# Linear attention with queries, keys and log decays projected in transposed form, block totals summed on VectorE, and the two-half products ordered tile by tile

## The chip, the cores and the metric

The kernel runs on one core of a Trainium2 chip. The metric is the device time in microseconds (us) of one execution; lower is better. TensorE does the matrix products, VectorE and ScalarE the arithmetic on rows, GpSimd some helpers, and SyncE issues all transfers.

## The reference, cut to what matters

One step of a two-layer backbone. In each layer a projection `h @ w_in` feeds three branches (grouped-query attention, gated linear attention, latent attention), their gates, and a merge. The change is in the linear attention (four heads, key width 64, value width 128, two directions, 1024 latent and 128 context tokens):

```python
qg = qg.reshape(bsz, n, GLA_HEADS, GLA_DK) * (GLA_DK ** -0.5)
la_f = jax.nn.log_sigmoid((rf @ p['w_gla_decay_fwd'] + p['b_gla_decay_fwd']))
la_b = jax.nn.log_sigmoid((rb @ p['w_gla_decay_bwd'] + p['b_gla_decay_bwd']))
...
def step(s, inp):
    qc, kc, vc, gc = inp
    cum = jnp.cumsum(gc, axis=1)
    last = cum[:, -1]
    o_inter = jnp.einsum('bchk,bhkv->bchv', qc * jnp.exp(cum), s)
    decay = jnp.exp(jnp.where(mask, cum[:, :, None] - cum[:, None, :], -jnp.inf))
    att = jnp.einsum('bihk,bjhk,bijhk->bhij', qc, kc, decay)
    s_new = jnp.exp(last)[..., None] * s + jnp.einsum('bjhk,bjhv->bhkv', kc * jnp.exp(last[:, None] - cum), vc)
```

## The kernel before

Tokens are nine tiles of 128. Every large product is made of three TensorE matmuls (`mm3`, lines 85 to 87), on a high and a low part of each factor. A layer runs in stages.

**Projection units.** `nat` puts tokens on partitions: a unit of 256 columns of `w_in` is 9 tiles x 8 k-steps x 3 matmuls with 256 moving columns. `trn` puts features on partitions: a unit of 128 columns is 3 chunks x 8 x 3 matmuls with 384 moving columns. `gla_unit` 0 and 1 make queries and keys with `nat`, 2 and 3 the values, all written to the scratch tensor `glas`. `decay` makes the log decays with tokens on partitions, and `decay2` finishes them and stores them in `las`.

**The scan.** `t_unit` makes the transposed gate projections (36 a layer). Class `Gla` hands out the linear attention of four heads in small steps, one after each twelve `mm3` matmuls of a `t_unit`, until the heads are done. Two chains of heads run side by side, the second `LAG` steps behind. Later `t_unit`s run without the scan, so the scan's TensorE work is added to that of the `t_unit`s, which does not depend on it.

A head (`head`, line 713) keeps rows of a tile with keys on partitions: the half `up` (partitions 0 to 63) and the half `dn` (64 to 127), one for each direction. It loads `la` and `qk`; line 735 multiplies the decays with the constant `blk` to get the totals of blocks of 1, 2, 4, up to 128 tokens, and lines 738 and 739 exponentiate them into `one` and `tot`; lines 751, 754 and 755 transpose queries and keys into `zb` and `za`. Then come six levels of widening blocks: line 793 for widths 1 to 16, line 809 for 32, line 820 for 64. In each, products of the `up` half go to a PSUM bank from `pst` and those of the `dn` half to a bank from `acc`; `join` then multiplies `za` and `zb` by the block decays on VectorE. The order of the first kind was:

```python
for pc, ks, qs, rows, f in ((banks[0], za, zb, up, 1), (banks[1], zb, za, dn, 0)):
    for t in range(NT):
        for b, bs in enumerate(quarters):
```

Line 837 turns the keys back into `kh` with tokens on partitions, line 847 makes the states' updates, lines 869 and 871 the output, line 885 transposes it.

**The rest.** Attention follows, then the merge and the output projection. The order on each engine is set by a scheduler from the order of the code and its own estimates; the engines run their lists in order, and the pools (three PSUM banks `f` for the units, two `acc`, three `pst`) set when a result's room is free. A matmul on full 32-bit data stands as two rows in the trace, one of `mm3` as one.

Of the kernel before, what the change touches and what calls it, by code (L numbers as in the profile page):

```python
# [20 lines left out]
P = 128  # L21
# [7 lines left out]
NCH = 3  # L29
# [17 lines left out]
def hybrid_step(ctx, tc, a):  # L47
# [174 lines left out]
    with ExitStack() as st:  # L222
        xs = enter(st, "hx0", 2)
        xT = xs.tile([P, KD, T], F32, tag="xT", name="xT", bufs=1)
        for t in range(NT):
            x32 = xs.tile([P, D], F32, tag="x", name="x", bufs=3)
            sp.dma_start(x32, x_rows(0, t))
            for hf, pt in to_t(pa["pst"], x_norm(xs, x32)):
                (act.copy, dve.tensor_copy)[hf](xT[:, hf * 4:hf * 4 + 4, t * P:(t + 1) * P], pt)
        loads = []  # L230
        for hf in range(2):
            def load(k):
                w = xs.tile([P, 2, 512], F32, tag="wm", name="wm", bufs=4)
                src = a["w_mod"][0, k * P:(k + 1) * P, 0:2 * D].rearrange("p (j c) -> p j c", j=2)
                loads.append(sp.dma_start(w, src[:, :, 512 * hf:512 * (hf + 1)]))
                return w.rearrange("p j c -> p (j c)")

            for step in mod_steps(0, [(j, 512 * hf, 512) for j in range(2)], pa[("f", "acc")[hf]], xs, load):
                step()
            if hf:  # L240
                last = loads[-1]
                with tc.issue_after(loads[9].ins):
                    first = load_unit(0, QG, pool)
# [21 lines left out]
    for l in range(DEPTH):  # L265
# [10 lines left out]
        glas = dr.tile([P, NT, 1024], F32, tag=f"glas{l}", name="glas")  # L276
        las = dr.tile([P, NT, 512], F32, tag=f"las{l}", name="las")
# [38 lines left out]
        with ExitStack() as st:  # L316
# [3 lines left out]
            def gla_unit(i, beside=None):  # L320
                hi, lo = first if l == 0 and i == 0 else load_unit(l, QG + 256 * i, dve)
                for t in range(NT):
                    if l or i:
                        pc = accf()
                    elif t % 2 == 0:
                        pair = (accf if t < 6 else pa["acc"])()
                        pc = pair
                    else:
                        pc = pair[:, 256:]
                    nat(pc[:, :256], t, hi, lo)  # L330
                    z = zp.tile([P, 256], F32, tag="zg", name="zg")
                    act.activation(z, pc[:, :256], AF.Copy, scale=1.0 if i else 0.125)  # L332
                    sp.dma_start(glas[:, t, 256 * i:256 * (i + 1)], z)
                    if beside:
                        beside(t)
                    elif i:
                        tick()

            gla_unit(0)
# [33 lines left out]
            u = n1.tile([P, NT, 512], F32, tag="u", name="u")  # L373
            mn = n1.tile([P, NT, 512], F32, tag="mn", name="mn")
# [3 lines left out]
            def decay(t):  # L378
                pc = accf()
                pe.matmul(pc, lhsT=rT[:, t * P:(t + 1) * P], rhs=wd.rearrange("p h b d -> p (h b d)"),  # L380
                          start=True, stop=True)
                act.activation(u[:, t], pc, AF.Abs)
                act.activation(u[:, t], u[:, t], AF.Exp, scale=-1.0)
                dve.tensor_scalar(mn[:, t], pc, 0.0, 1.0 / 16.0, op0=ALU.min, op1=ALU.mult)
# [10 lines left out]
            def decay2(t):  # L395
                rope_key(t, kr[:, t])
                if t % 3 == 2:
                    ts = slice(t - 2, t + 1)
                    act.activation(u[:, ts], u[:, ts], AF.Ln, bias=1.0)
                    dve.scalar_tensor_tensor(mn[:, ts], u[:, ts], -1.0 / 16.0, mn[:, ts], op0=ALU.mult, op1=ALU.add)  # L400
                    sp.dma_start(las[:, ts], mn[:, ts])

            gla_unit(1, decay)
            gla_unit(2, decay2)
            gla_unit(3)
# [112 lines left out]
        def t_unit(nm, c0, i, fill=None, beside=None):  # L518
            hi, lo = wunit(KD, P, [(0, P, a["w_in"][l, :, c0 + P * i:c0 + P * (i + 1)])], dve if beside else pool)
            for ch in range(NCH):  # L520
# [5 lines left out]
                if nm[0] != "m":  # L526
# [5 lines left out]
        env = dict(small=small, ident=ident, identr=identr, rstd=rstd, tri=tri, msk=msk,  # L532
                   twos=twos, wp=wp, wunit=wunit, cosm=cosm, sinm=sinm, split=split, mm3=mm3, glas=glas, las=las,
# [134 lines left out]
class Gla:  # L668
# [7 lines left out]
    def __init__(self, st, tc, enter, a, l, e):  # L676
# [7 lines left out]

        self.blk = self.g1.tile([P, 2 * P - 1], F32, tag="blk", name="blk")
        for w in BLOCKS:
            self.nc.vector.tensor_tensor(self.blk[:, OFF[w]:OFF[w] + P // w], e["tri"][:, 0, w - 1::w],
                                         e["tri"][:, 2, 0::w], op=ALU.mult)
# [24 lines left out]
    def head(self, h):  # L713
        nc, e, a, l, g1, g2, wide = self.nc, self.e, self.a, self.l, self.g1, self.g2, self.wide
        pe, act, dve, pool, sp = nc.tensor, nc.scalar, nc.vector, nc.gpsimd, nc.sync
        acc, pst, ident, blk = e["acc"], e["pst"], e["ident"], self.blk
# [3 lines left out]
        la = wide([NT, P], "la")  # L720
        sp.dma_start(la, e["las"][:, :, P * h:P * h + P])
        qk = wide([NT, 2, 64], "qk")
        for b in range(2):
            sp.dma_start(qk[:, :, b], e["glas"][:, :, 256 * b + 64 * h:256 * b + 64 * h + 64])
# [3 lines left out]
        one = wide([NT, P], "one")  # L728
        tot = wide([NT, P - 1], "tot")
        for t0 in range(0, NT, 2):  # L730
            n = min(2, NT - t0)
            pt = pst()[:, :n * (2 * P - 1)]
            for i in range(n):
                for rows in (up, dn):
                    pe.matmul(pt[rows, i * (2 * P - 1):(i + 1) * (2 * P - 1)], lhsT=la[:, t0 + i, rows], rhs=blk,  # L735
                              start=True, stop=True)
            pv = tiles(pt, n)
            act.activation(one[:, t0:t0 + n], pv[:, :, 0:P], AF.Exp)
            act.activation(tot[:, t0:t0 + n], pv[:, :, P:], AF.Exp)
            if t0 % 4:  # L740
                yield
        decay = lambda w: tot[:, :, OFF[w] - P:OFF[w] - P + P // w]
        yield

        za = wide([NT, P], "za")
        zb = wide([NT, P], "zb")
        for t0 in range(0, NT, 3):
            pa, pb = acc(), pst()
            for t in range(3):
                c = slice(t * P, (t + 1) * P)  # L750
                pe.transpose(pb[:, c], qk[:, t0 + t].rearrange("p b d -> p (b d)"), ident)
            for t in range(3):
                c = slice(t * P, (t + 1) * P)
                pe.matmul(pa[up, c], lhsT=qk[:, t0 + t, 1], rhs=ident, start=True, stop=True)
                pe.matmul(pa[dn, c], lhsT=qk[:, t0 + t, 0], rhs=ident, start=True, stop=True)
            act.copy(zb[:, t0:t0 + 3], tiles(pb[:, 0:3 * P], 3))
            act.copy(za[:, t0:t0 + 3], tiles(pa[:, 0:3 * P], 3))
            yield
# [14 lines left out]
        sp.dma_start(vn, e["glas"][:, :, 512 + P * h:512 + P * h + P])  # L773
# [5 lines left out]
        def join(w):  # L779
            d = one if w == 1 else decay(w)  # L780
            d = d.rearrange("p t (n f) -> p t n f", f=2)
# [24 lines left out]
        for b, bs in enumerate(quarters):  # L806
            ks, qs, rows = ((za, zb, up), (zb, za, dn))[b % 2]
            for t in range(NT):
                pe.matmul(banks[b % 2][bs, t * 32:t * 32 + 32], lhsT=ks[rows, t, bs], rhs=qs[rows, t, quarters[b ^ 1]],
                          start=True, stop=True, tile_position=(rows.start, 32 * b))  # L810
# [5 lines left out]
        for t0, n in ((0, 5), (5, 4)):  # L816
            banks = [pst()[:, 0:n * 64], acc()[:, 0:n * 64]]
            for pc, ks, qs, rows, other in ((banks[0], za, zb, up, dn), (banks[1], zb, za, dn, up)):
                for t in range(n):
# [13 lines left out]
        for t0, n in ((0, 4), (4, 4), (8, 1)):  # L833
            pc = pst()[:, 0:n * P]
            for t in range(n):
                for x, r in ((za, up), (zb, dn)):
                    pe.matmul(pc[:, t * P + r.start:t * P + r.stop], lhsT=x[:, t0 + t], rhs=ident[:, r],  # L837
                              start=True, stop=True)
            act.copy(kh[:, t0:t0 + n], tiles(pc, n))
            if t0 != 4:  # L840
                yield
# [642 lines left out]
```

## Time and profile before

| what | value |
|---|---|
| median of 3 runs | 3094.7 us (3093.02 to 3095.74) |
| the profiled execution's own time | 3095.74 us |
| its span, first to last instruction | 3094.0 us |
| TensorE busy | 3038.7 us, 98% |
| VectorE busy | 1579.4 us, 51% |
| ScalarE busy | 1154.8 us, 37% |
| scan of layer 0, and of layer 1 | about 366 to 728 us, and 1872 to 2234 us |

The span is 1.7 us shorter than the execution. Matmuls are pipelined and their ends are modelled, so that the length of one is not its cost: its cost is the distance to the start of the next.

### The profile page before, as it was taken

The numbers are of one execution on the slowest core, as the hardware profiler recorded it, in microseconds if no ns is written. First come the engines' busy times: TensorE is split into PE (matmuls) and PEld (weight loads), VectorE is DVE, ScalarE is ACT, GpSimd is POOL, SyncE is SP. The second block draws the span as 40 slices with busy tenths as digits, with TensorE's granted clock in tenths as the row PEclk, the third lists the DMA queues.
The fourth block names the chain that finished last, engine by engine and source line by source line (L and its number), as shares of the span: only waits on it lengthen the run. The fifth ranks groups of instructions, "written<-read, shape, count | busy, mean of one in ns | idle before, by whom it ended". The sixth has DMA issues, their size and how long they took to land.

```text
span 3094.0 us, 63128 instructions
## 1 busy us (share of the span) xinstructions
PE 3038.7 (98%) x25776; PEld 2673.5 (86%) x25776; DVE 1579.4 (51%) x2789; ACT 1154.8 (37%) x2412; POOL 750.2 (24%) x780
## 2 busy tenths in 40 slices
PE   7999999999999999999999999999999999999998
PEld 5989999999999666699899999999999976667997
DVE  5325543332078667757542473433213876786562
ACT  5523433333212565522345343333331245554121
POOL 3124300002200555500331460000130125553012
PEclk8999999999999999999999999999999999999999
DMA  7565522326343432186433444232463442214843
GB/s 238 175 191 160 142 76 82 100 82 187 112 119 102 133 94 78 33 258 210 152 102 116 119 114 122 88 96 75 123 178 98 123 140 91 78 52 139 276 140 109
DMA packets 389347, 394.72 MB, mean 128 GB/s; under 512 B 53740, under 2 KB 333804, under 8 KB 388928
## 3 DMA queue, kind: packets, MB, share of 16 engines
q1 hardware_dynamic: 389056, 390.67, 41.4%
q8 instruction: 203, 3.33, 0.5%
q14 instruction: 88, 0.72, 0.1%
HBM read 258.07 MB, written 113.64 MB: 120 GB/s over the span
## 4 chain that ended last, share of the span: by engine, by line
PE 93%; DVE 3%; ACT 1%; DMA 1%; issue 1%; SPq 0%; POOL 0%; ACTq 0%; DVEq 0%; POOLq 0%
PE f L85 18%; PE f L87 18%; PE f L86 18%; PE acc L1347 4%; PE acc L86 4%; PE acc L85 3%; PE acc L87 3%; PE pst L1089 3%; PE s L1214 2%; PE s L1215 2%; PE s L1172 1%; PE pst L735 1%; PE pst L837 1%; PE s L1174 1%; PE s L1173 1%; PE pst L793 1%
## 5 line engine op out<-in xcount | busy, mean ns | idle before, releaser
L85 PE MATMUL f<-big,whi 128*128 128x384 f32 x1776 | 609.1, 343 | 0.8 <-ACT zg L332 0.5
L87 PE MATMUL f<-big,wlo 128*128 128x384 f32 x1776 | 602.4, 339 | 0.7 <-issue 0.7
L86 PE MATMUL f<-big,whi 128*128 128x384 f32 x1776 | 600.4, 338 | 0.0
L85 PE MATMUL f<-whi,big 128*128 128x256 f32 (+1 forms) x1352 | 394.4, 292 | 1.2 <-ACT big L98 0.8
L87 PE MATMUL f<-whi,big 128*128 128x256 f32 (+1 forms) x1352 | 394.1, 292 | 0.8 <-DVE big L99 0.6
L86 PE MATMUL f<-wlo,big 128*128 128x256 f32 (+1 forms) x1352 | 392.7, 291 | 0.7 <-POOL wlo L99 0.7
L85 PEld LDWEIGHTS f<-big,whi 128*128 128x128 f32 x1776 | 333.7, 188 | 8.5 <-issue 6.4
L87 PEld LDWEIGHTS f<-big,wlo 128*128 128x128 f32 x1776 | 333.4, 188 | 3.9 <-issue 3.3
L86 PEld LDWEIGHTS f<-big,whi 128*128 128x128 f32 x1776 | 333.9, 188 | 1.8 <-issue 1.5
L99 DVE TENSOR_TENSOR wlo<-raw,whi 128x1024 fp32r<-128x1024 f32 (+3 forms) x116 | 141.7, 1222 | 348.7 <-ACT whi L98 186.2
L1102 ACT ACTIVATE pr<-s 128x512 f32<-128x512 f32 x440 | 247.8, 595 | 184.8 <-PE s L1215 111.7
L1107 POOL TENSOR_TENSOR sm<-sm,pr 128x512 f32<-128x512 f32 x192 | 264.9, 1393 | 179.8 <-DVE sm L1107 92.6
L85 PEld LDWEIGHTS f<-whi,big 128*128 128x128 f32 x1352 | 254.5, 188 | 15.6 <-issue 7.9
L87 PEld LDWEIGHTS f<-whi,big 128*128 128x128 f32 x1352 | 254.6, 188 | 7.3 <-DVE big L99 1.3
L86 PEld LDWEIGHTS f<-wlo,big 128*128 128x128 f32 x1352 | 254.6, 188 | 6.6 <-POOL wlo L99 1.2
L98 ACT CAST whi<-raw 128x1024 fp32r<-128x1024 f32 (+2 forms) x150 | 154.3, 1029 | 282.3 <-PE f L86 242.7
L1091 DVE TENSOR_REDUCE nm<-pst 128x1 f32<-128x384 f32 x480 | 239.5, 551 | 33.1 <-PE pst L1089 22.8
L99 POOL TENSOR_TENSOR wlo<-raw,whi 128x1024 fp32r<-128x1024 f32 x34 | 81.5, 2397 | 403.9 <-ACT whi L98 395.0
L1107 DVE TENSOR_TENSOR sm<-sm,pr 128x512 f32<-128x512 f32 x144 | 132.5, 924 | 87.7 <-POOL sm L1107 50.0
L525 ACT ACTIVATE g<-f 128x384 f32<-128x384 f32 x144 | 70.4, 489 | 285.3 <-PE f L87 197.6
L92 POOL TENSOR_SCALAR rm<-oss 128x9 f32<-128x9 f32 x8 | 1.7, 207 | 614.9 <-ACT sq L875 614.9
L99 DVE TENSOR_TENSOR lo<-pr,hi 128x512 fp32r<-128x512 f32 (+1 forms) x148 | 145.4, 1005 | 3.6 <-ACT hi L98 3.4
(329 smaller groups left out, 6063.2 us busy)
## 6 DMA issues: line engine op xcount, KB each, us to landing
raw<-in_w_in SPq DMA_DIRECT2D x108, 512.0 KB
gtm<-g SPq DMA_DIRECT2D x144, 192.0 KB
sg<-gtm SPq DMA_DIRECT2D x144, 192.0 KB
wm<-in_w_mod SPq DMA_DIRECT2D x48, 512.0 KB
big<-y SPq DMA_DIRECT2D x96, 192.0 KB
glas<-zg SPq DMA_DIRECT2D x72, 128.0 KB
gqT<-stg SPq DMA_DIRECT2D x36, 256.0 KB
gqa<-gqT SPq DMA_DIRECT2D x36, 256.0 KB
```

The lines of the kernel that those rows point to most:

```text
L85: pe.matmul(out, lhsT=lh, rhs=rh, start=first, stop=False)
L86: pe.matmul(out, lhsT=lh, rhs=rl, start=False, stop=False)
L87: return pe.matmul(out, lhsT=ll, rhs=rh, start=False, stop=last)
L98: act.copy(hi, src)
L99: lo_eng.tensor_tensor(lo, src, hi.bitcast(F32), op=ALU.subtract)
L525: act.activation(th, pc[:, :CH], AF.Tanh, scale=0.5)
L1089: r = nc.tensor.matmul(pc[:, :CH], lhsT=q[:, t * P:(t + 1) * P], rhs=k[:, j * CH:(j + 1) * CH], start=True, stop=True)
L1091: nc.vector.reduce_max(nm[:, t, j:j + 1], pc[:, :CH], axis=AX.X)
L1102: self.nc.scalar.activation(pr, pc, AF.Exp, scale=scale)
L1107: eng.tensor_tensor(s_, x, y, op=ALU.add)
L1214: pe.matmul(pc, lhsT=self.kah[g][:, ks], rhs=qa, start=True, stop=False)
L1347: after = nc.tensor.matmul(po[64 * j:64 * j + 64], lhsT=at.gv[:, kt, g], rhs=pr, start=j not in begun, stop=kt == GROUPS[-1][0])
```

## The change

Queries and keys of a head come from one `trn` unit (64 query and 64 key columns, `qk_unit`, four a layer), with features on partitions, and are stored in `qkT`. The decays are made with features on partitions too (12 matmuls of 384 columns for 9 of 512). A head loads `one`, `zb` and `za` as it needs them; the constant `blk`, its products and the transposes are gone. Block totals are made by seven additions on VectorE, each from pairs of the one before, and two ScalarE instructions exponentiate all of them. In the levels, and where the keys are turned back, the tile loop is outside and the half inside; the keys are turned back with 64 rows at a time, one bank for each half.

```diff
-            gla_unit(0)
+            def qk_unit(h, beside):
+                hi, lo = wunit(KD, P, [(64 * i, 64, a["w_in"][l, :, c + 64 * h:c + 64 * h + 64])
+                                       for i, c in enumerate((QG, KG))], dve)
+                for ch in range(NCH):
+                    pc = accf()
+                    trn(pc[:, :CH], ch, hi, lo)
+                    z = n2.tile([P, CH], F32, tag="zt", name="zt")
+                    act.activation(z[0:64], pc[0:64, :CH], AF.Copy, scale=0.125)
+                    dve.tensor_copy(z[64:128], pc[64:128, :CH])
+                    sp.dma_start(qkT[:, h, ch * CH:(ch + 1) * CH], z)
+                    beside(NCH * h + ch)
...
-            gla_unit(1, decay)
-            gla_unit(2, decay2)
-            gla_unit(3)
+            v_unit(1, key)
+            for h in range(4):
+                qk_unit(h, finish)
...
-                    pe.matmul(pt[rows, i * (2 * P - 1):(i + 1) * (2 * P - 1)], lhsT=la[:, t0 + i, rows], rhs=blk,
-                              start=True, stop=True)
...
+        for w in BLOCKS[1:]:
+            x = decay(w // 2).rearrange("p t (n f) -> p t n f", f=2)
+            dve.tensor_tensor(decay(w), x[:, :, :, 0], x[:, :, :, 1], op=ALU.add)
+        for x in (one, tot):
+            act.activation(x, x, AF.Exp)
...
-            for pc, ks, qs, rows, f in ((banks[0], za, zb, up, 1), (banks[1], zb, za, dn, 0)):
-                for t in range(NT):
+            for t in range(NT):
+                for pc, ks, qs, rows, f in ((banks[0], za, zb, up, 1), (banks[1], zb, za, dn, 0)):
...
-                for x, r in ((za, up), (zb, dn)):
-                    pe.matmul(pc[:, t * P + r.start:t * P + r.stop], lhsT=x[:, t0 + t], rhs=ident[:, r],
-                              start=True, stop=True)
+                for pc, x, r in zip(banks, (za, zb), (up, dn)):
+                    pe.matmul(pc[:, t * 64:t * 64 + 64], lhsT=x[r, t0 + t], rhs=ident[r, r], start=True, stop=True)
```

The order on TensorE shows it at three places of layer 0, before first and then changed; L85 to L87 are the `mm3` matmuls of the gate units. The start of the first head, before:

```order
L735 MATMUL pst<-blk,la 64x255 x12
L87 MATMUL f<-big_102,wlo 128x384
L85 MATMUL f<-big_102,whi 128x384
L754 MATMUL acc<-ident,qk 64x128
L755 MATMUL acc<-ident,qk 64x128
L754 MATMUL acc<-ident,qk 64x128
L755 MATMUL acc<-ident,qk 64x128
L754 MATMUL acc<-ident,qk 64x128
L755 MATMUL acc<-ident,qk 64x128
L735 MATMUL pst<-blk,la 64x255 x6
```

The same place in the changed kernel (L762 is the old L767, L787 the old L793):

```order
L85 MATMUL f<-big_104,whi 128x384
L86 MATMUL f<-big_105,whi 128x384
L87 MATMUL f<-big_104,wlo 128x384
L762 MATMUL pst<-zb,za 32x32 x36
L787 MATMUL acc<-za,zb 32x16 x36
L85 MATMUL f<-big_104,whi 128x384
L86 MATMUL f<-big_105,whi 128x384
```

The products with `blk` and the transposes are gone, and a head begins with its first product. The width of 64 of the first head, before:

```order
L87 MATMUL f<-big_102,wlo 128x384
L820 MATMUL pst<-zb,za 64x64 x5
L820 MATMUL acc<-za,zb 64x64 x5
L735 MATMUL pst<-blk,la 64x255 x8
L820 MATMUL acc<-za,zb 64x64 x4
L85 MATMUL f<-big_102,whi 128x384
```

And in the changed kernel, where L814 is the old L820:

```order
L814 MATMUL pst<-zb,za 64x64
L814 MATMUL acc<-za,zb 64x64
L814 MATMUL pst<-zb,za 64x64
L814 MATMUL acc<-za,zb 64x64
L814 MATMUL pst<-zb,za 64x64
L814 MATMUL acc<-za,zb 64x64
L814 MATMUL pst<-zb,za 64x64
L814 MATMUL acc<-za,zb 64x64
```

The halves `up` (to `pst`) and `dn` (to `acc`) now take turns, one matmul each, without a break. The keys of the first head turned back, before:

```order
L837 MATMUL pst<-ident,za 128x64
L751 MATMUL pst<-ident,qk 128x128 x3
L837 MATMUL pst<-ident,za 128x64
L837 MATMUL pst<-ident,zb 128x64
L837 MATMUL pst<-ident,za 128x64
L837 MATMUL pst<-ident,zb 128x64
```

And changed, where L831 is the old L837:

```order
L87 MATMUL f<-big_104,wlo 128x384
L831 MATMUL pst<-ident,za 128x64 x2
L831 MATMUL acc<-ident,zb 128x64 x2
L831 MATMUL pst<-ident,za 128x64
L831 MATMUL acc<-ident,zb 128x64
L831 MATMUL pst<-ident,za 128x64
```

They took turns between `za` and `zb` already, each with all 128 rows; now each uses one half's 64 rows, and the banks differ.

## Rows read from the trace of the kernel before

**Rows 1.** The page: busy time of TensorE, its share of the span, instructions.

```profile
PE 3038.7 (98%) x25776; PEld 2673.5 (86%) x25776; DVE 1579.4 (51%) x2789; ACT 1154.8 (37%) x2412; POOL 750.2 (24%) x780
```

**Rows 2.** Chain of waits in the scan, 366 to 728 us: shares by line.

```profile
by line: PE f L85 22.5%; PE f L87 21.7%; PE f L86 21.5%; PE pst L735 4.9%; PE pst L837 4.3%; PE pst L793 3.9%; PE acc L793 3.7%; PE acc L754 2.4%; PE acc L869 2.4%; PE pst L847 2.3%; PE acc L871 2.0%; PE acc L820 1.2%; PE pst L809 1.2%; PE 
```

**Rows 3.** Stretches: both scans, projections of layer 0; length, busy per engine, PEclk, DMA.

```profile
366.00:728.00 362.00, 360.74 (x5617) 335.97 (x5616) 128.89 (x224) 119.84 (x300) 15.03 (x12) 1.00 0.30 91
1872.00:2234.00 362.00, 360.70 (x5619) 335.83 (x5619) 128.68 (x224) 119.64 (x300) 15.04 (x12) 1.00 0.30 91
92.00:354.00 262.00, 262.00 (x2249) 239.59 (x2248) 118.03 (x284) 104.50 (x258) 90.98 (x155) 1.00 0.57 172
```

**Rows 4.** Timeline of TensorE: `nat` matmuls; start us, length us, instruction.

```profile
141.16 0.28 PE L85 MATMUL f<-whi,big 128*128 128x256 f32 x1
...
143.18 0.28 PE L87 MATMUL f<-whi,big 128*128 128x256 f32 x1
```

**Rows 5.** The same timeline: `trn` matmuls.

```profile
358.83 0.33 PE L85 MATMUL f<-big,whi 128*128 128x384 f32 x1
...
360.91 0.33 PE L85 MATMUL f<-big,whi 128*128 128x384 f32 x1
```

**Rows 6.** The same timeline: totals of the first head.

```profile
366.55 2.80 PE L735 MATMUL pst<-blk,la 128*64 128x255 f32 x24
369.28 0.44 PE L87 MATMUL f<-big,wlo 128*128 128x384 f32 x1
369.56 0.34 PE L85 MATMUL f<-big,whi 128*128 128x384 f32 x1
```

**Rows 7.** The same timeline: transposes of queries and keys.

```profile
370.10 0.27 PE L754 MATMUL acc<-ident,qk 128*64 128x128 f32 x1
370.10 0.27 PE L755 MATMUL acc<-ident,qk 128*64 128x128 f32 x1
370.21 0.27 PE L754 MATMUL acc<-ident,qk 128*64 128x128 f32 x1
```

**Rows 8.** The same timeline: keys turned back.

```profile
435.37 0.39 PE L837 MATMUL pst<-ident,zb 128*128 128x64 f32 x2
435.59 0.39 PE L837 MATMUL pst<-ident,za 128*128 128x64 f32 x2
435.82 0.39 PE L837 MATMUL pst<-ident,zb 128*128 128x64 f32 x2
```

**Rows 9.** The same timeline: width 64, where `up` ends and `dn` begins.

```profile
425.75 0.62 PE L820 MATMUL pst<-zb,za 64*64 64x64 f32 x7
426.15 0.27 PE L820 MATMUL acc<-za,zb 64*64 64x64 f32 x1
...
426.26 0.22 PE L820 MATMUL acc<-za,zb 64*64 64x64 f32 x1
426.26 0.22 PE L820 MATMUL pst<-zb,za 64*64 64x64 f32 x1
426.32 0.22 PE L820 MATMUL acc<-za,zb 64*64 64x64 f32 x1
426.32 0.22 PE L820 MATMUL pst<-zb,za 64*64 64x64 f32 x1
```

**Rows 10.** The same timeline: width 32, a run on one half.

```profile
419.39 0.54 PE L809 MATMUL acc<-za,zb 64*32 64x32 f32 x12
419.75 0.21 PE L809 MATMUL pst<-zb,za 64*32 64x32 f32 x1
```

**Rows 11.** The same timeline: a narrow level, where `up` ends and `dn` begins.

```profile
392.17 0.77 PE L793 MATMUL pst<-zb,za 64*32 64x16 f32 x70
...
392.77 0.18 PE L793 MATMUL pst<-zb,za 64*32 64x16 f32 x1
392.77 0.20 PE L793 MATMUL acc<-za,zb 64*32 64x16 f32 x1
392.79 0.18 PE L793 MATMUL pst<-zb,za 64*32 64x16 f32 x1
392.79 0.80 PE L793 MATMUL acc<-za,zb 64*32 64x16 f32 x70
393.53 0.44 PE L86 MATMUL f<-big,whi 128*128 128x384 f32 x1
```

**Rows 12.** Groups on VectorE in the scan: a `join` with strided halves.

```profile
L784 DVE TENSOR_TENSOR za<-za,tot 128x576 f32<-128x576 f32 x24 | 18.2, 760 | 24.4 <-PE acc L820 12.4 <-PE pst L820 8.2 <-PE acc L809 3.7
```

More of the change, by code (lines that the diff above doesn't have):

```diff
@@ L242, in hybrid_step @@
                 with tc.issue_after(loads[9].ins):
-                    first = load_unit(0, QG, pool)
+                    first = load_unit(0, VG, pool)
             for t0, t1 in ((0, 1), (1, 3), (3, 6), (6, 8), (8, 9)):
@@ L318, in hybrid_step, with v_unit @@
             n2 = enter(st, f"n2{l}", 3)
-            def gla_unit(i, beside=None):
-                hi, lo = first if l == 0 and i == 0 else load_unit(l, QG + 256 * i, dve)
+            def v_unit(i, beside=None):
+                hi, lo = first if l == 0 and i == 0 else load_unit(l, VG + 256 * i, dve)
                 for t in range(NT):
@@ L371, in rope_key, with decay, key @@
                 act.copy(ksT[:, t * P:(t + 1) * P], pt[0:64, 0:P])
[L373 to L374 removed]
+            u = n1.tile([P, 4, T], F32, tag="u", name="u")
+            mn = n1.tile([P, 4, T], F32, tag="mn", name="mn")
             kr = n1.tile([P, NK, 32], F32, tag="kr", name="kr")
             sp.dma_start(kr[:, 0], a["cache_mla_krope"][l])
[L378 to L384 removed]
+            def decay(i):
+                h, sl = i // NCH, slice(i % NCH * CH, (i % NCH + 1) * CH)
+                pc = accf()[:, :CH]
+                pe.matmul(pc, lhsT=wd[:, h].rearrange("p b d -> p (b d)"), rhs=rT[:, sl], start=True, stop=True)
+                act.activation(u[:, h, sl], pc, AF.Abs)
+                act.activation(u[:, h, sl], u[:, h, sl], AF.Exp, scale=-1.0)
+                dve.tensor_scalar(mn[:, h, sl], pc, 0.0, 1.0 / 16.0, op0=ALU.min, op1=ALU.mult)
+            def key(t):
+                for i in range(t * 4 // 3, (t + 1) * 4 // 3):
+                    decay(i)
                 pk = pst()
@@ L715, in head @@
         pe, act, dve, pool, sp = nc.tensor, nc.scalar, nc.vector, nc.gpsimd, nc.sync
-        acc, pst, ident, blk = e["acc"], e["pst"], e["ident"], self.blk
+        acc, pst, ident = e["acc"], e["pst"], e["ident"]
         tiles = lambda x, n: x.rearrange("p (t x) -> p t x", t=n)
         up, dn = slice(0, 64), slice(64, P)
[L720 to L724, printed above, removed]
+        one = wide([NT, P], "one")
@@ L725, in head @@
+        sp.dma_start(one, tiles(e["las"][:, h], NT))
+        zb = wide([NT, P], "zb")
+        sp.dma_start(zb, tiles(e["qkT"][:, h], NT))
+        za = wide([NT, P], "za")
+        for x, y in ((up, dn), (dn, up)):
+            sp.dma_start(za[x], tiles(e["qkT"][y, h], NT))
         yield
-        one = wide([NT, P], "one")
+        yield
         tot = wide([NT, P - 1], "tot")
[L730 to L734, printed above, removed]
-                    pe.matmul(pt[rows, i * (2 * P - 1):(i + 1) * (2 * P - 1)], lhsT=la[:, t0 + i, rows], rhs=blk,
-                              start=True, stop=True)
[L737 to L741, printed above, removed]
@@ L742, in head @@
-        decay = lambda w: tot[:, :, OFF[w] - P:OFF[w] - P + P // w]
-        yield
[L745 to L758, printed above, removed]
+        decay = lambda w: one if w == 1 else tot[:, :, OFF[w] - P:OFF[w] - P + P // w]
@@ L772, in head @@
         vn = wide([NT, P], "vn")
[L773 removed]
+        sp.dma_start(vn, e["gvn"][:, :, P * h:P * h + P])
         yield
@@ L779, in join @@
         def join(w):
-            d = one if w == 1 else decay(w)
-            d = d.rearrange("p t (n f) -> p t n f", f=2)
+            d = decay(w).rearrange("p t (n f) -> p t n f", f=2)
             for x, f in ((za, 0), (zb, 1)):
@@ L805, in head @@
         banks = [pst()[:, 0:NT * 32], acc()[:, 0:NT * 32]]
-        for b, bs in enumerate(quarters):
-            ks, qs, rows = ((za, zb, up), (zb, za, dn))[b % 2]
-            for t in range(NT):
+        for t in range(NT):
+            for b, bs in enumerate(quarters):
+                ks, qs, rows = ((za, zb, up), (zb, za, dn))[b % 2]
                 pe.matmul(banks[b % 2][bs, t * 32:t * 32 + 32], lhsT=ks[rows, t, bs], rhs=qs[rows, t, quarters[b ^ 1]],
@@ L817, in head @@
             banks = [pst()[:, 0:n * 64], acc()[:, 0:n * 64]]
-            for pc, ks, qs, rows, other in ((banks[0], za, zb, up, dn), (banks[1], zb, za, dn, up)):
-                for t in range(n):
+            for t in range(n):
+                for pc, ks, qs, rows, other in ((banks[0], za, zb, up, dn), (banks[1], zb, za, dn, up)):
                     pe.matmul(pc[rows, t * 64:t * 64 + 64], lhsT=ks[rows, t0 + t, rows], rhs=qs[rows, t0 + t, other],
@@ L832, in head @@
         kh = wide([NT, P], "kh")
-        for t0, n in ((0, 4), (4, 4), (8, 1)):
-            pc = pst()[:, 0:n * P]
+        for t0, n in ((0, 5), (5, 4)):
+            banks = [pst()[:, 0:n * 64], acc()[:, 0:n * 64]]
             for t in range(n):
-                for x, r in ((za, up), (zb, dn)):
-                    pe.matmul(pc[:, t * P + r.start:t * P + r.stop], lhsT=x[:, t0 + t], rhs=ident[:, r],
[L838 to L841, printed above, removed]
+                for pc, x, r in zip(banks, (za, zb), (up, dn)):
+                    pe.matmul(pc[:, t * 64:t * 64 + 64], lhsT=x[r, t0 + t], rhs=ident[r, r], start=True, stop=True)
+            for pc, r in zip(banks, (up, dn)):
+                act.copy(kh[:, t0:t0 + n, r], tiles(pc, n))
+            yield
         act.copy(zb[dn], za[dn])
```

37 lines of the change are left out of this document (18 added, 19 removed).

## The prediction

> **What bounds the kernel now.** Read the page first: TensorE is busy 98% of the span [rows 1]. Since ends of matmuls are modelled, that alone proves little, so read next what ended last. In the scan's stretch the chain of waits is TensorE nearly throughout: two thirds are the matmuls of the gate units, and the scan's own lines follow, with no wait of any size among them [rows 2]. [...] So TensorE's list is the time. What leaves it is gained and what joins it is lost, as long as the other engines keep up. Its price is the distance between starts, which I read from the timeline.
>
> **What leaves TensorE.** The products with `blk`: 4.9% of a scan's 362 us [rows 2, 3] is 17.7 us, 35 us for two layers. The timeline agrees: 24 rows in 2.73 us (366.55 to 369.28), 0.114 us each, two rows to a matmul [rows 6]; 9 tiles x 2 halves x 2 rows x 8 heads are 288 rows, 33 us. The transposes of lines 754 and 755: a pair of rows each 0.11 us [rows 7], 144 pairs, 16 us; the chain puts 2.4% on line 754, 17 us in two layers [rows 2]. I take 16.5. Line 751 loads 128 weight columns per matmul like line 837, whose rows are 0.11 us apart [rows 8]; 72 rows are 8 us. Together 60 us. Nothing hides these rows, so all of it is gain, if nothing comes in their place.
>
> **The halves in turn, width 64 and 32.** At width 64 seven `up` rows take 0.40 us, 0.057 each. Where `up` gives way to `dn`, rows of both halves start together, at 426.26 and again at 426.32: a pair each 0.06 us where one half alone gives a single row [rows 9]. So the two halves of the array do work at the same time once the order lets them. 2 halves x 9 tiles x 2 rows x 8 heads are 288 rows x 0.057 = 16.4 us; half is 8.2. Width 32: 12 rows in 0.36 us, 0.030 each [rows 10]; 576 rows are 17.3 us, half is 8.6. Here the old order changed halves after each 9 tiles, so a little of this is had already; I take 8. The bounds of each are nothing and the half.
>
> **The keys turned back.** 4.3% of the chain [rows 2] is 15.6 us a layer, 31 us in all; rows are 0.11 us apart [rows 8] though only 64 columns move (width 64 moves as many in 0.057 us [rows 9]), so loading 128 weight columns sets the pace. The number of matmuls stays; each now uses one half's rows and the halves take turns. No row before has two halves over the same output columns, so the gain lies between nothing and a half, 15.5 us. The nearest row is width 64, where halves overlap completely, weight loads too; I take the half.
>
> **The narrow levels.** Line 793 is 3.9% and 3.7% of the chain [rows 2], 27.5 us a layer, 55 us in all, the largest item. Here 70 rows start within 0.60 us, 0.0085 each, and at the change of halves, where both are in flight, a pair starts each 0.02 us, no faster than before [rows 11]. Something other than the array seems to set this pace, such as the rate at which instructions come. The gain is between nothing and a half, 27 us; by these rows it is near the lower end, and I take 5, for the beginning of each block.
>
> **Fewer interruptions.** After a block of the scan the second gate matmul starts 0.28 us after the first (369.28 to 369.56) instead of 0.17 [rows 5, 6]: 0.1 us for each return. In the order of instructions there were 164 such blocks, and are 110: 54 x 0.1 = 5 us. As blocks also hide a part of their own start, I take 3.
>
> [...]
>
> **The units.** `nat` rows are 17 in 2.02 us, 0.119 us [rows 4], `trn` rows 12 in 2.08 us, 0.173 us [rows 5]. Two units of 216 are 51.3 us; four of 72 are 49.9 us. That is 1.4 us a layer; I take 2 for both, between 0 and 3. The decays move the same 4608 columns: nothing.
>
> **What is added off TensorE.** Seven additions a head on VectorE. The first makes 576 elements from strided pairs, as a `join` does in 0.76 us [rows 12]; each next one has half as many. Sized by that, less than 1.6 us without fixed costs; with those, I estimate 2.5. Four heads add 10 us to 129 in the scan [rows 3], where two thirds of the time is spare: nothing. Without that cover it would be 20 us in both layers. ScalarE loses ten small exponentials a head and gets two long ones; it was busy 120 of 362 us. SyncE gets two weight loads for each unit with rows of 256 bytes, and loads three tensors a head instead of two; DMA engines stood at 0.30 in the scan and 0.57 in the projections [rows 3]. Queued behind such a load on SyncE are stores of the units' results; those have three buffers in their pool and are not waited for as long as a unit's 12.5 us (72 rows) covers the load. I allow 4 us for new small waits.
>
> **Sum.** 60 + 8 + 8 + 15.5 + 5 + 3 + 2 - 4 = 97.5 us, from the profiled execution's 3095.7 (span 3094.0): 2998. That execution lay 1.0 us over the median of the runs, 3094.7; against this the forecast is 2997.
>
> **The rivals.**
> *Keys don't overlap* (A): halves over the same columns load their weights one after the other. Then 15.5 us stay: 3012.
> *Narrow levels overlap too* (B): if the pace of line 793 is the array's after all, 22 us more go: 2975. For it: it is the same change as at width 64. Against it: the pairs at 392.77 [rows 11]. [...]
> *No overlap anywhere* (C): what rows 9 show is a property of the change-over and does not last. Only what leaves counts, 60 + 3 + 2 - 4 = 61 us: 3034.
> *A wait takes the place* (D): the first products of a head now wait for its load, seven additions in a row and two exponentials over 1152 and 1143 elements. If each head exposes 2.5 us of additions and about as much of exponentials, 5 x 8 = 40 us come back: 3037. For it: the additions stand in VectorE's queue among the gates' evacuations, which hold the three `f` banks. Against it: heads run side by side with twelve steps of lead, and the old order's similar chain cost TensorE next to nothing [rows 3].
> *Slower* (E): each change of halves drains the array. The changes are about 680 at line 787, 280 at 803, 130 at 814 and 140 at 831. If each cost a matmul's own length (0.18 us in rows 11, 0.21 in rows 10, 0.22 in rows 9, 0.27 in rows 7) that would be 122 + 59 + 29 + 38 = 248 us more, against 61 gained: 3282. It decides from 0.05 us per change. Against it: rows 9 and 11 show a change of halves at no cost.
> *Nothing gained* (F): new waits eat all of it; some 100 us, 12 a head, would have to appear on a chain that shows 1.3 us of idle time in a scan [rows 3].
>
> **How the numbers follow.** Forecast 0.54, alone 2986 to 3008 (line 793 between 0 and 10, waits between 0 and 12); A 0.13; B 0.11; C 0.07; D 0.09; E 0.03; F 0.03. The forecast, A and B and their spread hold 0.78; the range 2970 to 3025 takes these in, with the milder part of D. Within 0.2% (6 us, about what can be told from no change) is F, 0.03, and slower is E, 0.03; all else is faster, 0.94.
>
> **What would show it.** Right: lines 735, 751, 754 and 755 gone from TensorE; at lines 814 and 803 starts of `pst` and `acc` rows in pairs, 18 rows of a half within some 0.5 us of a level's 1.1; line 831 in pairs 0.11 us apart; line 787 at 0.008 us a row still; the granted clock at 1.00 in the scan; idle time in TensorE's stretches as small as before; the scan's stretch over about 50 us earlier, with the gate units after it as many us later. Wrong: line 831 at 0.11 us per row (A); line 787 at 0.004 (B); pairs that don't last (C); TensorE idle before lines 762 and 787 with VectorE's additions as releaser (D); starts 0.2 us apart where halves change (E).

## The result, and the profile after

| kernel | median us (lowest to highest, runs) | ratio to before, 95% interval |
|---|---|---|
| before, same chip | 3094.4 (3093.0 to 3095.7, 4) | 1 |
| changed | 3025.9 (3023.5 to 3031.6, 4) | 0.978 [0.976, 0.980] |

The change gained 68.5 us where 97.5 were forecast. 3025.9 lies just over the range (2970 to 3025). The profiled execution took 3031.58 us, the longest of the four, with a span of 3029.8; against the one of before it gained 64.2 us.

The page of the changed kernel, busy times, and shares of the chain by engine. They answer to [rows 1]:

```profile
PE 2947.8 (97%) x24846; PEld 2606.7 (86%) x24846; DVE 1603.7 (53%) x2855; ACT 1131.4 (37%) x2314; POOL 762.1 (25%) x786
...
PE 90%; DVE 3%; DMA 2%; issue 2%; ACT 2%; SPq 0%; POOL 0%; ACTq 0%; DVEq 0%; POOLq 0%
```

"issue" is time in which TensorE stood still and waited for nothing that the profile shows. Look for it again in the chain of the scan's first 362 us, which answers to [rows 2]:

```profile
by line: PE f L85 24.2%; PE f L87 24.0%; PE f L86 23.7%; PE pst L787 4.4%; PE acc L787 3.3%; PE acc L862 2.7%; PE pst L840 2.3%; PE pst L831 2.2%; PE acc L864 2.1%; issue 1.8%; PE pst L814 1.3%; PE pst L878 1.3%; PE pst L916 1.3%; PE acc L8
```

The products with `blk` and the transposes are gone, and the keys turned back (line 831) stand at 2.2% instead of 4.3%. But 1.8% is "issue", 6.5 us. The stretches, as in [rows 3], say how TensorE fared in the two scans:

```profile
344.00:706.00 362.00, 355.54 (x5562) 342.08 (x5562) 158.01 (x312) 129.56 (x293) 40.44 (x32) 0.99 0.45 133
1815.00:2177.00 362.00, 347.49 (x5519) 332.99 (x5518) 158.10 (x312) 127.91 (x289) 37.22 (x31) 0.99 0.44 128
```

Idle time was 1.3 us in each scan before; it is 6.5 and 14.5 now. Of the 14.5 us in the second scan's stretch, 3.2 are waits with a name (engine, line, who it waited for: us in total, times, longest):

```profile
PE acc L85 <- DMA xT<-qlT: 1.9, 2, 1.1
PE pst L787 <- DVE zb L765: 1.3, 1, 1.3
```

The first is for loads of the latent attention, the second for VectorE's product ahead of a narrow level. All other waits of note in the two stretches stand as "issue". The halves did what was forecast. The timeline of TensorE (start us, length us, instruction), first width 32, then width 64, then the keys turned back, answering to [rows 10], [rows 9] and [rows 8]:

```profile
407.52 0.19 PE L803 MATMUL pst<-zb,za 64*32 64x32 f32 x1
407.52 0.19 PE L803 MATMUL acc<-za,zb 64*32 64x32 f32 x1
407.53 0.19 PE L803 MATMUL pst<-zb,za 64*32 64x32 f32 x1
...
413.52 0.22 PE L814 MATMUL pst<-zb,za 64*64 64x64 f32 x1
413.53 0.22 PE L814 MATMUL acc<-za,zb 64*64 64x64 f32 x1
413.58 0.22 PE L814 MATMUL pst<-zb,za 64*64 64x64 f32 x1
...
419.18 0.27 PE L831 MATMUL pst<-ident,za 64*128 64x64 f32 x1
419.19 0.27 PE L831 MATMUL acc<-ident,zb 64*128 64x64 f32 x1
419.29 0.27 PE L831 MATMUL pst<-ident,za 64*128 64x64 f32 x1
```

A pair starts each 0.06 us at width 64 and each 0.11 us with the keys, where before a single row took that long. So what took the rest of the forecast gain? Here is one place where TensorE stands still, in the chain of the changed kernel in order of time (start us, length us, what):

```profile
496.67 0.73 PE acc L787 x57
497.40 0.37 PE f L85
497.77 0.36 PE pst L787 x31
498.13 1.65 issue
499.78 0.53 PE pst L787 x40
```

The stop falls into the middle of one narrow level: 31 rows, then nothing for 1.65 us, then the rest. The matmuls before and after it write the same bank from the same operands, so no data can be late.

What does coincide is found among the transfers. The page counts them by queue and kind (packets, MB, share):

```profile
q1 hardware_dynamic: 375584, 395.39, 43.0%
q8 instruction: 195, 3.19, 0.4%
```

Each of the 195 packets on the queue q8 has 16,384 bytes; TensorE's records count 50,080 (49,692 matmuls and weight loads, the rest mainly semaphore instructions), which is 256.8 a packet; at 256 the packets hold 49,920. I take as a stop each place after the first 80 us where the next matmul is over 0.55 us later than the median for its line and shape and no wait is named. In the profile of before there are 4, of 3.0 us in all; in that of the changed kernel 13, of 19.5 us. In all 13 a packet lands 1.3 to 1.6 us before TensorE goes on. And if TensorE's instructions are numbered from the start, the instruction that ends a stop has a number that is 193 or 194 over a multiple of 256, in all 13 and in the 4 of before: it is the first of a packet, and the packet that landed has the place in the queue that goes with that number. The packet in the rows above began at 497.50, took 0.93 us, and 1.34 us later, at 499.78, its first instruction ran. It began when only 63 instructions were left to run. The packets of the stops are little slower than the others: 0.9 to 1.6 us, 1.2 in the median, where all 195 take 0.9 to 1.9 and 1.0 in the median.

### The profile page after: what moved, and what is told of

It is laid out like the page before. It is cut to its first block, busy times and chain, and to the rows that moved or that the text cites. A ratio compares the mean times of both kernels' runs of the same rounds, so it can differ in the third digit from the quotient of the medians.

```text
span 3029.8 us, 61204 instructions
## 1 busy us (share of the span) xinstructions
PE 2947.8 (97%) x24846; PEld 2606.7 (86%) x24846; DVE 1603.7 (53%) x2855; ACT 1131.4 (37%) x2314; POOL 762.1 (25%) x786
## 4 chain that ended last, share of the span: by engine, by line
PE 90%; DVE 3%; DMA 2%; issue 2%; ACT 2%; SPq 0%; POOL 0%; ACTq 0%; DVEq 0%; POOLq 0%
PE f L85 18%; PE f L87 18%; PE f L86 18%; PE acc L1340 4%; PE acc L86 4%; PE acc L85 3%; PE acc L87 3%; PE pst L1082 3%; PE s L1207 2%; PE s L1208 2%; PE s L1165 1%; PE pst L787 1%; PE s L1166 1%; PE s L1167 1%; PE pst L437 1%
## 5 line engine op out<-in xcount | busy, mean ns | idle before, releaser
L85 PE MATMUL f<-big,whi 128*128 128x384 f32 x1968 | 672.8, 342 | 1.5 <-ACT zg L333 1.5
L87 PE MATMUL f<-big,wlo 128*128 128x384 f32 x1968 | 668.3, 340 | 2.4 <-issue 2.4
L86 PE MATMUL f<-big,whi 128*128 128x384 f32 x1968 | 667.0, 339 | 2.9 <-issue 2.9
L85 PEld LDWEIGHTS f<-big,whi 128*128 128x128 f32 x1968 | 371.8, 189 | 5.0 <-ACT zg L333 2.1
L86 PEld LDWEIGHTS f<-big,whi 128*128 128x128 f32 x1968 | 372.0, 189 | 3.5 <-issue 2.9
L87 PEld LDWEIGHTS f<-big,wlo 128*128 128x128 f32 x1968 | 371.7, 189 | 2.9 <-issue 2.3
L99 DVE TENSOR_TENSOR wlo<-raw,whi 128x1024 fp32r<-128x1024 f32 (+2 forms) x110 | 134.4, 1222 | 364.5 <-PE f L86 224.6
L85 PE MATMUL f<-whi,big 128*128 128x256 f32 (+1 forms) x1064 | 314.4, 296 | 2.7 <-ACT zg L333 2.0
L87 PE MATMUL f<-whi,big 128*128 128x256 f32 (+1 forms) x1064 | 313.5, 295 | 0.7 <-DVE big L99 0.6
L86 PE MATMUL f<-wlo,big 128*128 128x256 f32 (+1 forms) x1064 | 312.5, 294 | 1.4 <-POOL wlo L99 1.4
L85 PEld LDWEIGHTS f<-whi,big 128*128 128x128 f32 x1064 | 201.2, 189 | 18.1 <-issue 7.0
L87 PEld LDWEIGHTS f<-whi,big 128*128 128x128 f32 x1064 | 201.0, 189 | 6.6 <-DVE big L99 1.3
L86 PEld LDWEIGHTS f<-wlo,big 128*128 128x128 f32 x1064 | 201.2, 189 | 6.2 <-POOL wlo L99 1.9
L1340 PE MATMUL acc<-pr,gv 128*64 128x512 f32 x576 | 137.7, 603 | 0.0
```

The source lines that it names most:

```text
L85: pe.matmul(out, lhsT=lh, rhs=rh, start=first, stop=False)
L86: pe.matmul(out, lhsT=lh, rhs=rl, start=False, stop=False)
L87: return pe.matmul(out, lhsT=ll, rhs=rh, start=False, stop=last)
L99: lo_eng.tensor_tensor(lo, src, hi.bitcast(F32), op=ALU.subtract)
L1340: after = nc.tensor.matmul(po[64 * j:64 * j + 64], lhsT=at.gv[:, kt, g], rhs=pr, start=j not in begun, stop=kt == GROUPS[-1][0])
```

## The experiments

*Theory one*: instructions come in packets, one ahead at most; where TensorE uses up 256 instructions faster than the next packet comes, it stands still. A narrow level has 288 in 1.2 to 1.5 us. How often it stops hangs on where the borders between packets fall. *Theory two*: the new order of halves and banks causes the stops.

**The order alone, and stops moved on purpose.** Four kernels. `order_alone` is the kernel before with the loops exchanged in the three kinds of levels, like this one:

```diff
-            for pc, ks, qs, rows, other in ((banks[0], za, zb, up, dn), (banks[1], zb, za, dn, up)):
-                for t in range(n):
+            for t in range(n):
+                for pc, ks, qs, rows, other in ((banks[0], za, zb, up, dn), (banks[1], zb, za, dn, up)):
```

> The kernel before with one edit: in the three kinds of levels the tile loop is outside and the half inside; projections, totals, transposes and the keys stay as they were, so no instruction comes or goes. Theory one (TensorE's instructions come in packets of 16,384 bytes, 256 instructions each, and TensorE stands still where it uses up a packet faster than the next one lands; the stops hang on where the borders of packets fall): the order by itself costs no stops. Widths 32 and 64 gain what their rows gained in the changed kernel, 10 and 5 us, the narrow levels nothing: 3094 - 15 = 3079, and stops without a wait of about 3 us as before. Theory two (taking turns between halves and banks causes the stops itself): some 15 us of stops appear in the levels, 3094. By the sizes of the prediction (8 + 8 + 5) it would be 3073.

`before_moved` and `after_moved` repeat one product 32 times, 128 instructions more, which moves all later borders:

```diff
-                pe.matmul(pc[bs, t * 32:t * 32 + 32], lhsT=za[up, t, bs], rhs=zb[up, t, bs],
+                for _ in range(33 if l + h + t + b == 0 else 1): pe.matmul(pc[bs, t * 32:t * 32 + 32], lhsT=za[up, t, bs], rhs=zb[up, t, bs],
```

> The kernel before with one edit: the first product of the first head of layer 0 is repeated 32 times (same result), 128 instructions more, so that all later borders of packets fall half a packet earlier in the program. The repeats cost about 64 rows x 0.03 = 2 us. Theory one (instruction supply): the kernel before owed its few stops (3.0 us in 4 places) to where the borders fell; moved by 128, the borders fall into dense stretches more often, and by the spacing of its matmuls the stops come to 9 to 14 us: about 3104. Theory two (the new order causes the stops): this kernel has the old order, so only the repeats are added: 3096.

> The changed kernel with the same edit: the first product of the first head of layer 0 is repeated 32 times, 128 instructions more. Theory one (instruction supply): the stops move to other blocks, and the count of instructions at which they end, taken modulo 256 in the old numbering, moves by 128; by the spacing of the matmuls layer 0 has about 2 us more of them and layer 1 about 5 us less: 3026 + 2 - 3 = 3025. Theory two: the stops stay at the blocks where they were, and the time rises by the repeats alone: 3028.

`levels_split` is the changed kernel with this in the narrow levels' tile loop:

```diff
+                if t == 4:
+                    yield
```

> The changed kernel with one edit: each narrow level is given out in two steps, five tiles and then four, so that gate matmuls stand between the halves of its 288 instructions (72 matmuls of two rows, each with its weight load). Theory one (instruction supply): a packet of 256 no longer fits into one dense stretch; the stops without a wait, 19.5 us in 13 places in the profile of the changed kernel, fall under 5 us; some 40 returns more at 0.1 us cost 4: 3026 - 15 + 4 = 3015. Theory two (the turns between halves cause the stops): the stops stay, 3030.

| kernel | median us | ratio to before | stops, us |
|---|---|---|---|
| order_alone | 3078.5 | 0.9954 [0.9940, 0.9968] | 2, 1.5 |
| before_moved | 3107.6 | 1.0047 [1.0034, 1.0059] | 8, 8.5 |
| after_moved | 3019.1 | 0.9756 [0.9742, 0.9769] | 10, 10.8 |
| levels_split | 3013.5 | 0.9737 [0.9724, 0.9751] | 3, 2.8 |

Theory two falls. The new order alone brings no further stop and gains 15 us, as theory one expected. The old order gets more stops, 8.5 us of them instead of 3.0, from nothing but 128 more instructions ahead of it; here is one in the chain of `before_moved`:

```profile
464.64 0.69 PE pst L793 x55
465.33 0.53 PE acc L793 x31
465.86 1.40 issue
467.26 0.31 PE acc L793 x15
```

So the kernel before owed its quiet scans to the places where its borders fell. `before_moved` lost 13.8 us, 3.6 more than theory one's sum: the two scans, up to attention's first product, became 10.0 us longer, 5.5 of it in stops, about 2 in the repeats, and about 1 in the gate matmuls behind the stop shown here, where the granted clock was 0.57 from 468 to 472 us; the rest, 1.5, is not in them. In `after_moved` the stops end at 193 or 194 again, in its own numbering, which is 65 or 66 in the old one: they moved by 128, to other blocks. Layer 1 has 3.7 us of them instead of 12.4, more than the 5 less expected; layer 0 has 7.1 as before, not 2 more. And with gate matmuls inside the narrow levels the stops nearly vanish; the scans of `levels_split` answer to the two rows above:

```profile
346.00:708.00 362.00, 361.34 (x5568) 345.12 (x5567) 149.23 (x284) 122.46 (x274) 27.00 (x22) 1.00 0.41 123
1812.00:2174.00 362.00, 360.36 (x5560) 343.99 (x5559) 147.71 (x283) 122.09 (x274) 26.41 (x21) 1.00 0.40 123
```

**The parts of the change.** `keys_alone` and `narrow_alone` are the kernel before with one part each, as the change's diff shows it; `rest_alone` is the changed kernel with both taken back and widths 32 and 64 too.

> The kernel before with one edit: the keys are turned back as in the changed kernel, 64 rows at a time, halves in turn, one bank for each half. The count of instructions stays. By the prediction's term: 15.5 us less, 3078. By the spacing of the rows of line 831 in the changed kernel (65 ns against 111 ns for the keys' blocks with their returns): 13 us less, 3081. Rival A of the prediction (halves over the same columns load their weights one after the other): no change, 3094.

> The kernel before with one edit: in the narrow levels (widths 1 to 16) the tile loop is outside and the half inside; the count of instructions stays. By the prediction's term: 5 us less, 3089. By the rows of the changed kernel, where a narrow level has the same 10.6 ns a row as before: nothing, 3094 within 3. Rival B (the array sets this pace): 27 us less, 3067.

> The changed kernel with all orders of loops of before in the levels and the keys turned back as before: only the products with blk, the transposes and the units differ from the kernel before. By the prediction's terms 60 + 3 + 2 us less 4 for waits: 3033, without stops. Theory one (instruction supply; the count of instructions is that of the changed kernel, so borders fall about where they fell there, and narrow levels are as dense in the old order): 8 to 20 us of stops come on top, 3041 to 3053. Theory two (taking turns between halves causes the stops): no stops beyond the 3 us of before, 3033.

`keys_alone` took 3088.0 us, 0.9983 [0.9974, 0.9992]: 5.8 us gained, between rival A and the term, and a miss of both expectations. Its profile is better than its median: the scans are 9.5 us shorter with 0.7 us more of stops, 10.2 by themselves. In its timeline 226 neighbours of different halves are 56 ns apart on the mean, which is full overlap, but 44 rows stand behind a row of their own half, 118 ns apart, as the scheduler ordered them there. In the changed kernel all 278 neighbours take turns, 56 ns. So rival A is refuted, and the size depends on the order around it. The 9.5 us of the profiles and the 5.8 of the medians differ by which executions were profiled: that of before took 3095.7 us, 2.0 over the median of before in this comparison, and that of `keys_alone` 3086.3, 1.7 under its own. What makes one execution of a kernel differ from the next by this much is not shown. `narrow_alone` took 3093.9, 1.0002 [0.9993, 1.0011]: nothing, and rival B is refuted. `rest_alone` took 3045.2, 0.9844 [0.9831, 0.9858], with 11 stops of 13.9 us in the old order: theory one again.

**ScalarE's tables.** The changed kernel lost 3.6 us between the first decay product of layer 1 and the first transpose of line 437. ScalarE and TensorE there (start us, length us, engine, and in brackets the idle time before it and who ended it):

```profile
1608.03 1.28 ACT L417 ACT_TABLE_LOAD   x1
1609.32 1.16 ACT L417 ACTIVATE u<-u 128x1152 f32<-128x1152 f32 x1
1610.39 0.35 ACT L333 COPY zg<-f 128x256 f32<-128x256 f32 x1
...
1610.80 0.58 PE L85 MATMUL f<-whi,big 128*128 128x256 f32 x1 [2.03 <-ACT zg L333]
```

The logarithm of a head (line 417) is issued as soon as its exponentials are done, among those of the next head, so ScalarE loads function tables to and fro, and a copy that frees an `f` bank is late. `split_ln` adds to `levels_split`:

```diff
-                act.activation(u[:, h, sl], u[:, h, sl], AF.Exp, scale=-1.0)
+                ex.append(act.activation(u[:, h, sl], u[:, h, sl], AF.Exp, scale=-1.0))
...
-                    act.activation(u[:, h], u[:, h], AF.Ln, bias=1.0)
+                    with tc.issue_after(ex[-1].ins):
+                        act.activation(u[:, h], u[:, h], AF.Ln, bias=1.0)
```

> The changed kernel with its narrow levels given out in two steps (as in the run levels_split, 3013.5 us) and a second edit: ScalarE's four logarithms of the decays are issued after the last of their exponentials. In the changed kernel ScalarE loads a function table 7 times among the projections of layer 1, 1.28 us each, as logarithms and exponentials alternate, and TensorE there waits 3.3 us for two of ScalarE's copies behind them; before there were 5 such loads and no such wait. If the loads are the cause, the stretch from the first decay product to the query units of layer 1 falls from 82.0 to 78.7 us: 3013.5 - 3.5 = 3010. If the copies are late for another reason, the stretch stays, 3013.5.

It took 3007.5 us, 0.9723 [0.9709, 0.9736], the fastest of all. The stretch went from 82.0 us in `levels_split` to 77.7 (78.7 before). In it ScalarE loads a table once:

```profile
L420 ACT ACTIVATE u<-u 128x1152 f32<-128x1152 f32 x4 | 4.3, 1156 | 0.0
...
L420 ACT ACT_TABLE_LOAD x1 | 1.3, 1283 | 0.0
```

In the changed kernel it loads one seven times there, and five times before. The edit moves the loads and the logarithms themselves out of the copies' way together; which of the two made the copies late is not separated.

**Spacing, and once more.** Both wider kernels have this edit, `spread` in the changed kernel, `split_spread` in `split_ln`:

```diff
-                if beside and k % 4 == 3:
+                if beside and (ch * KD + k) % 6 == 5:
```

> The changed kernel with one edit: a step of the scan after every 18 matmuls of a gate unit instead of every 12, so that the blocks stand further apart (3.1 us instead of 2.1) but each is as dense as before. If it is the narrow level itself that uses up a packet of 256 instructions too fast (288 instructions in 1.2 to 1.5 us), spacing takes away only those stops for which two blocks share a packet: 8 to 15 us of stops stay of 19.5, 3018 to 3026. If the nearness of blocks is what matters, the stops go as in the run levels_split, to about 3 us, 3011.

> The kernel of the run split_ln (3007.5 us; narrow levels in two steps, logarithms after the exponentials) with steps after every 18 matmuls instead of 12. Instruction supply: the stops of 2.6 us that were left there fall to 1 or less, nothing else changes: 3006, within 3 of 3007.5. Were the blocks' returns to the gate matmuls or waits for VectorE what is left, a wider spacing would give more than that: 3002 or less.

> The changed kernel once more, unchanged, for a second profiled execution. Instruction supply: stops end at the same counts of instructions, modulo 256, and mostly in the same blocks, since the borders are those of the program; their lengths differ with when each packet is asked for. 3026 within 4. Chance events of the memory would put them elsewhere.

`spread` took 3013.0, 0.9741 [0.9728, 0.9754], with 4 stops of 5.6 us: fewer than expected from dense levels alone, more than from splitting. Both the density of a block (a run of the scan's matmuls between two gate matmuls) and the distance to the next one count. `split_spread` missed by far: 3079.9, 0.9960 [0.9947, 0.9972]. In two stretches of its scans (345 to 707 and 1804 to 2166 us) TensorE is busy for 361.01 and 360.23 of 362 us; but the scan now lasts too long. Its last transpose of line 878's kind stands at 804 us instead of 685 in `split_ln`, and the latent attention's queries, which follow, have hardly a gate unit left to stand behind; that this is the reason is read from the order and the waits, no run tests it. Two stretches, one in each layer, and a group of waits in the first of them (engine, line, who it waited for: us in total, times, longest):

```profile
780.00:860.00 80.00, 62.03 (x359) 58.30 (x358) 20.46 (x52) 24.71 (x60) 21.60 (x17) 0.85 0.61 176
2280.00:2360.00 80.00, 62.56 (x374) 58.59 (x373) 25.42 (x63) 24.95 (x60) 23.89 (x19) 0.91 0.64 184
```

```profile
PE acc L85 <- DMA xT<-qlT: 10.8, 5, 5.2
```

TensorE is idle for 18.0 and 17.4 us and its granted clock is 0.85 and 0.91; in `split_ln` the same two stretches have 0.0 and 0.7 us of idle time at 1.00. This idle time is half of the 72 us between the two kernels; the lower granted clock, 0.983 on the mean of the whole execution against 0.996 in `split_ln`, stands beside it and is not added up.

`after_again` took 3021.5, 0.9768 [0.9755, 0.9782]. 12 of its 13 stops (17.4 us) stand at the numbers of the first profile. Its median is 4.4 us under the first one, just outside what was expected; it lies inside the prediction's range, and 24 us over its forecast all the same. Over all 13 profiled executions there are 81 such stops, and 79 of them end at 193 or 194 over a multiple of 256; the other two stand in `split_spread` at 844 and 847 us, among those late queries, and are counted to no packet.

## Why the prediction was wrong, point by point

The accounts are those of the two profiled executions: 64.2 us gained. The stretches from a layer's first decay product to its first product of attention became 66.8 us shorter, both layers together; what lies outside them became 2.6 longer.

- *60 for what leaves, 3 for interruptions, 2 for units*: right as a sum; no run parts them. `rest_alone` is 52.3 us shorter in these stretches. Without its stops beyond those of before (10.9), its wait for ScalarE (3.4) and 1.6 for a slow clock that is 68, against 65.
- *Widths 64 and 32, 8 each*: the sum is right, and luck has a part in it. The scans of `order_alone` are 18.1 us shorter, 1.5 of it in fewer stops: 16.6. But by the distances between rows width 32 gains some 11 us (from 28 to 9 ns a row on the mean, within its blocks), more than the half that was given as its bound, and width 64 some 3 to 5. In the order of TensorE before, 98 of 268 neighbours at width 64 already stood on different halves, which the prediction did not take off; and at width 32 the new order changes the quarter of the columns along with the half, which it did not count. What each of the two changes brings there is not separated.
- *Keys turned back, 15.5*: mechanism right, 10 to 15 by the rows (288 rows, from 108 ns to 56 ns on the mean in the changed kernel, are 15; alone 10 in its profile, 5.8 by the medians). The ends of its ten blocks cost some 2 us more than before, which the sum does not count: the first row of line 831 starts 0.26 us after the gate matmul ahead of it where that of line 837 started 0.18 after, and the way back to the second gate matmul takes some 0.14 more.
- *Narrow levels, 5*: wrong. In 36 of 40 levels they take turns now, at 8.7 ns a row on the mean within a block, the same as before, and `narrow_alone` shows nothing. The prediction read in [rows 11] that the array doesn't set this pace, and granted 5 all the same.
- *No wait of VectorE's additions (D), no cost where halves change (E)*: right. A head's seven additions take 752, 458, 299, 232, 195, 180 and 171 ns on the mean, 2.3 us, where 2.5 was estimated. The scan waits for no addition, only once, 1.3 us in layer 1, for the product of line 765 that follows them, and changes of halves cost nothing at 0.06 us a pair.
- *Minus 4 for new small waits*: this step failed. It looked only at waits for other engines and at queues of data. Of these, 3.6 us came for ScalarE and 3.2 in the second scan (1.9 for the loads of `xT`, 1.3 for line 765), not far from the 4. What it did not look at is the larger part: 16.5 us more of stops for instructions (19.5 against 3.0) and 6.4 us of slow clock behind them (below). With 2.6 us outside the stretches these are 32.3. The terms gave 96.5 by this account (64.2 + 32.3), against 101.5 before the allowance; the narrow levels' 5 make up that difference, and smaller misses of the other terms, up and down, lie inside it. `after_again`, counted the same way, gives some 98. And with the stops and ScalarE's waits nearly gone, `split_ln` took 3007.5 us, 10.5 over the forecast of 2997.

The slow clock is seen behind four of the five longest stops of the changed kernel, and behind one shorter one. Stretches from the end of three of them on; the third number from the end is the granted clock:

```profile
500.00:504.00 4.00, 4.00 (x52) 3.97 (x40) 3.77 (x10) 0.49 (x1) 0.00 (x0) 0.68 0.01 4
2001.80:2005.80 4.00, 3.97 (x16) 3.97 (x17) 1.37 (x2) 2.31 (x8) 0.05 (x1) 0.69 0.02 4
2040.40:2044.00 3.60, 3.57 (x17) 3.54 (x18) 1.73 (x3) 0.00 (x0) 0.00 (x0) 0.57 0.18 59
```

TensorE stood still for 1.8, 2.9 and 2.8 us ahead of these. The granted clock is 0.68, 0.69 and 0.57 in them, and where it is low gate matmuls start 0.32 us apart instead of 0.173 [rows 5]:

```profile
2041.20 0.52 PE L87 MATMUL f<-big,wlo 128*128 128x384 f32 x1
2041.52 0.52 PE L85 MATMUL f<-big,whi 128*128 128x384 f32 x1
```

The other two, 442.3 to 446.3 and 568.8 to 572.8 us, have 0.64 and 0.62. Five such stretches cost 6.4 us by that difference; the scans of before have none, with 1.00 throughout [rows 3].

The prediction's sentence on the bound, "TensorE's list is the time", held "as long as the other engines keep up". What didn't keep up was, for the most part, no engine but the supply of the list itself. The mark that was given for this, idle time as small as before, is the one that showed it.

Of the 195 packets of the changed kernel, 13 go with stops, of 19.5 us in all. In these 13 the packet began when 1 to 264 instructions were left, and over all 195 packets never when more than some 300 were, so that in this program little more than one packet was ahead.

What stays open: that the kernel before fell so well (its four stops, 3.0 us) is chance of position as far as `before_moved` shows; whether a packet could be asked for earlier was not tried. The parts, measured one by one, add up to 95 to 100 us, the whole to 96.5 or 98; closer than this they are not compared.

## What to carry to other kernels

Where a block of small matmuls uses up 256 instructions in less than some 3 us (an estimate from the stops above: 0.9 to 1.6 us for the packet, 1.3 to 1.6 until it runs), look for "issue" in TensorE's chain and number the instructions: if stops end at one remainder of 256, give the block out in pieces with long matmuls between them, but see first what cover the spread-out work takes from what comes after it. In `before_moved` and `after_moved` 128 instructions added ahead moved such stops, so that some 10 us between two versions of such a kernel can be a matter of position: `before_moved` lost 12 without its repeats, 5.5 of them in stops that the trace shows. When an edit splits work on ScalarE by heads, fence functions of different tables apart: `split_ln` has one table load where the changed kernel has seven, and the stretch took 77.7 us instead of 82.0.

## What was not expected of the hardware

- 128 harmless instructions made the kernel before 13.8 us slower, 0.47%, though they take about 2 us themselves.
- In the 13 stops of the changed kernel, a packet takes 0.9 to 1.6 us, and from its landing to its first instruction another 1.3 to 1.6 pass.
- Behind a stop of 1.8 us at 498 us, and one of 1.35 at 567, TensorE's granted clock was 0.68 (500 to 504 us) and 0.62 (568.8 to 572.8); behind one of 1.7 us at 1908 us it was 1.00 (1909.6 to 1913.6).
- Two halves overlap fully when they write the same output columns of different banks too: 56 ns a row against 108.
